# Two sequence blocks side by side through the mixers, and their w_out as seven block products

## The chip, the cores and the metric

The kernel runs on one core of a Trainium2 chip. The metric is the device time of one execution in microseconds (us), as the median of several. Profiled executions give a span (first to last instruction of the core), a little shorter than the device time.

## The reference

One decoder layer, batch 1, 2048 rows (tokens), width 1024, float32:

```
h = RMSNorm(x);  u = h @ W_in                        (1024 -> 3584)
gate_b, gate_c, v (512 each), x_r, g (1024 each) = split(u)
y_conv = gate_b * conv3(gate_c * v)                  (causal, per channel)
xr     = conv4(x_r) + bias                           (causal, per channel)
y_rnn  = RG-LRU(xr) * gelu(g)                        (16 heads of 64: two sigmoid gates
                                                      by block-diagonal products, then a scan)
x = x + concat[RMSNorm(y_conv), RMSNorm(y_rnn)] @ W_out    (1536 -> 1024)
x = x + relu(RMSNorm(x) @ W1)^2 @ W2                 (1024 -> 4096 -> 1024)
out = RMSNorm(x)
```

The scan and the convolutions run along the rows, so each block of rows needs the state that the block before left.

## The kernel before

The 2048 rows are four blocks of 512 (TB). A product is done in three passes: each factor is split into a rounded part (hi, on ScalarE) and a rest (lo, on VectorE, `split_into`, L180 to L182), and hi x hi, hi x lo and lo x hi are summed in PSUM. A matmul instruction takes 128x128 weights and 512 columns. PSUM has four tiles of 128x2x512, which all stages share.

Blocks are taken in pairs. The second pair (blocks 2 and 3) goes side by side: `pair_before_mlp` runs `mixers2`, then w_out, and both blocks form the halves of one matrix, so that seven products of half size replace eight (Strassen's form as Winograd wrote it; `ORDER` gives their order). For w_in and for w_out the kernel needs sums of the weights' quarters, as hi and lo parts. `prepare_sums` and `prepare_out_sums` make them one step at a time (`step`, the generator `background`) and put them in DRAM, in block 1's mixers (18 steps: `BG_UNITS`, `BG_STEPS`) and in the first pair's MLP. The MLP of each pair (`mlp`, lines L857 and L975) also uses seven products.

The first pair (blocks 0 and 1) goes one block after the other. `mixers(b, h)` walks through 14 units of w_in of 256 columns: x0 to x3 and g0 to g3 (recurrent), c0, c1, v0, v1, b0, b1 (conv). A unit is 48 matmuls (`mm_cols`, L240). `take` hands out a unit's pieces, loads and splits those two units ahead, and with `put_by` stores the split pieces in DRAM, from where block 1 and the second pair read them (`load_unit`, `In.load`). Between the units stand the recurrent chains, one for each pair of 128 channels (`pr` 0 to 3): `lru_take`, `lru_conv`, `lru_split`, `lru_gates` (12 small matmuls into `psri`, L692, then sigmoids), `lru_scan`. The first block's first three units are written out by hand before it (`start_x`, L486 to L546).

Meanwhile `next_part(b, n)` prepares the row factors of a later block: n = 0 to 3 load x (L1205) and square it (L1213), 4 takes the root, 6 forms a diagonal, 8 spreads it over the columns with two matmuls (`spread`, L449). `next_scale` multiplies the transposed x by the factors (L459) and `next_split` splits it into `h`.

`w_out_rows` and `w_out_conv` then multiply by w_out with the plain form: 12 groups of 24 matmuls in each block (`mm_rows`, L267), the factors of the norms put on the results on the rows' side. `turn` transposes the normed rows for the MLP (L1742).

`WOut.multiply` (L1889) is the seven-product w_out of the second pair. There the conv part's factor relative to the recurrent one is spread over the columns (`quotient`, `spread`), since both parts share a product.

Order: in `mixers` and the old w_out a planner orders each engine's instructions (program order is the priority; it takes what its cost model finds ready) and gives out the tile slots: 27 in `tp` (`temp`), 15 in `wp` (weights), 3 wide ones in `xp`, 2 in `hp`. In the second pair's part before the MLP, TensorE, ScalarE and VectorE are in program order, and in the MLP TensorE alone (`manual_schedule`). Nearly all transfers are issued in the queue of SP.

Of the kernel before, what the change touches and what calls it, by code (L numbers as in the profile page):

```python
# [15 lines left out]
P = 128  # L16
# [16 lines left out]
OUT_AHEAD = 2  # L33
# [7 lines left out]
BG_UNITS = 24  # L41
BG_STEPS = 2
# [22 lines left out]
def block_kernel(  # L65
# [5 lines left out]
    norm_mlp_g,  # L71
# [57 lines left out]
    def src_row(w, row):  # L129
        v = w[row : row + 256, :].rearrange("(j p) n -> p j n", p=P)  # L130
        return [v[:, 0:1, :], v[:, 1:2, :]], (P, 1, D)

    def src_quad(w, row):
        v = w[row : row + 512, :].rearrange("(h j p) n -> p h j n", p=P, j=2)
        return [
            v[:, i, :, 512 * c : 512 * c + 512] for i in range(2) for c in range(2)
        ], (P, 2, 512)

    units = []
    PAIRED = 2  # L140
    UNITS = ("x0", "g0", "x1", "c0", "g1", "x2", "v0", "g2", "x3", "b0", "g3", "c1", "v1", "b1")
    COLS = dict(x=COL_X, g=COL_G, c=COL_C, v=COL_V, b=COL_B)
    for b in range(PAIRED):
        for nm in UNITS:
            units.append((nm, src_col(w_in, COLS[nm[0]] + 256 * int(nm[1]))))
        for pr in range(4):
            units.append(("oB%d" % pr, src_row(w_out, 512 + 256 * pr)))
        for pr in range(2):
            units.append(("oA%d" % pr, src_row(w_out, 256 * pr)))
# [3 lines left out]
    NU = len(UNITS) + 6  # L153
    cache = {}

    def put_by(u, tiles):

        cache[units[u][0]] = []
        for part in tiles:
            row = []  # L160
            for t in part:
# [74 lines left out]
    def mm_cols(ps, w, h, j, lo=0, hi=TB, ks=range(KD)):  # L236
        for k in ks:
            pl = passes(w, h)
            for i, (ws, hs) in enumerate(pl):
                nc.tensor.matmul(  # L240
                    ps[:, j, lo:hi],
                    ws[k // 4][:, k % 4, j * P : (j + 1) * P],
                    hs[:, k, lo:hi],
# [3 lines left out]

    made = {}

    def col_unit(nm, h, ahead=AHEAD):  # L250
        if nm in made:
            return made.pop(nm)
        w = take(nm, ahead)
        if BG_UNITS <= cursor[0] < BG_UNITS + 9:
            for _ in range(BG_STEPS):
                step()
# [5 lines left out]

    def mm_rows(ps, y, w, j, t, first, final):
        pl = passes(y, w)
        for i, (ys, ws) in enumerate(pl):
            for half in range(2):
                nc.tensor.matmul(  # L267
                    ps[:, half, :],
                    ys[:, j, t * P : (t + 1) * P],
                    ws[j][:, 0, half * 512 : (half + 1) * 512],  # L270
                    start=first and i == 0,
                    stop=final and i == len(pl) - 1,
                )

# [123 lines left out]
    def norm_tile(b, t, g):  # L398
        ss = small("ss")
        rs = small("rs")[:, 0:1]  # L400
        xs = temp("xs")
        for i in range(2):
            nc.scalar.activation(
                xs[:, i, :], x_half(b, t, i), AF.Square, accum_out=ss[:, i : i + 1]
            )
        V.tensor_add(ss[:, 0:1], ss[:, 0:1], ss[:, 1:2])
        root = rstd_of(rs, ss[:, 0:1], 1)
        for i, sl in enumerate(HALF):
            V.scalar_tensor_tensor(xs[:, i, :], x_half(b, t, i), rs, g[:, sl], MUL, MUL)
        return xs, root  # L410

# [42 lines left out]
    def spread_rows(rs, n):  # L454
        return spread(diagonal(rs, n), n)

# [9 lines left out]

    def to_h(xs, h, t, parts=1):
        ps = psum("tps", (P, KD, P))
        for k in range(KD):
            nc.tensor.transpose(ps[:, k, :], xs[:, k // 4, k % 4 * P : (k % 4 + 1) * P], ident)  # L470
# [1958 lines left out]
```

## Time and profile before

| what | value |
|---|---|
| median of 3 runs | 2107.11 us (2106.87 to 2107.33) |
| profiled execution | 2106.28 us, span 2104.5 us |
| TensorE busy | 2096.0 us, 9396 matmuls |
| VectorE busy | 1603.7 us, 1848 instructions |
| ScalarE busy | 1104.2 us |
| transfers | 493 MB, 234 GB/s |
| granted TensorE clock | 0.999 |
| first block until its w_out ends | about 237 us |
| first pair until its MLP alone is left | about 486 us |

How to read it: a group of the profile is one line of the kernel on one engine with the tiles it writes and reads (out<-in), its count, its busy time in all, the mean of one, and the idle time of the engine just before its instructions with what ended it. A row of busy time by stretch gives the stretch, its length, the busy time of PE (TensorE matmul), PEld (weight load), DVE (VectorE), ACT (ScalarE) and POOL (GpSimd) with the instruction counts in brackets, the granted clock, the share of the DMA engines and GB/s; asked for one line, it shows the engines of that line only. Times of a chain start at the span's start.

### The profile page before, as it was taken

How to read it: one execution, taken by the hardware profiler on the slowest of the kernel's cores; microseconds unless marked ns; L12 is line 12 of the kernel's file. 1: busy time of each engine (PE TensorE's matmuls, PEld its weight loads, DVE VectorE, ACT ScalarE, POOL GpSimd, SP SyncE). 2: the span in 40 equal slices, each digit the busy share in tenths (PEclk: the TensorE clock that was granted, in tenths of full speed). 3: DMA queues.
4: the chain of work that ended last, by engine and by line, in shares of the span. 5: the costliest groups of instructions: out<-in, count | busy, mean ns of one | idle time of the engine just before them, and what ended most of it. 6: DMA issues, size and time to landing. Idle time of an engine off the chain costs nothing.

```text
span 2104.5 us, 25165 instructions
## 1 busy us (share of the span) xinstructions
PE 2096.0 (100%) x9396; PEld 1726.4 (82%) x9396; DVE 1603.7 (76%) x1848; ACT 1104.2 (52%) x1438; POOL 54.8 (3%) x71
## 2 busy tenths in 40 slices
PE   9999999999999999999999999999999999999998
PEld 7888888888888888888888887888888888888887
DVE  6889538858775777999997876785886765887776
ACT  6875447726554554444455888234764333333344
POOL 0110000000000000000000100000000000000000
PEclk9999999999999999999999999999999999999999
DMA  9988889743667778689564656775343355854432
GB/s 340 333 307 326 316 327 352 283 174 111 239 251 255 274 286 333 236 315 338 210 259 169 216 207 230 266 266 208 121 166 134 145 185 208 310 178 155 140 120 81
DMA packets 204762, 492.98 MB, mean 234 GB/s; under 512 B 15840, under 2 KB 80352, under 8 KB 204640
## 3 DMA queue, kind: packets, MB, share of 16 engines
q1 hardware_dynamic: 203040, 486.65, 63.9%
q10 hardware_dynamic: 1568, 4.72, 0.6%
q8 instruction: 74, 1.21, 0.2%
q14 instruction: 48, 0.39, 0.1%
q0 software_dynamic: 32, 0.00, 0.0%
HBM read 324.59 MB, written 166.72 MB: 233 GB/s over the span
## 4 chain that ended last, share of the span: by engine, by line
PE 99%; DVE 1%; ACT 0%; issue 0%; POOL 0%; ACTq 0%; POOLq 0%
PE up L857 42%; PE dn L975 28%; PE po L267 6%; PE ps_g L240 4%; PE wo_x L1889 3%; PE ps_x L240 3%; PE ps_v L240 2%; PE ps_b L240 2%; PE ps_c L240 2%; PE wo_w L1889 2%; PE wo_y L1889 1%; PE tps L1742 1%; PE psri L1498 1%; PE psri L692 1%; PE start_x L518 1%; PE start_x L240 1%
## 5 line engine op out<-in xcount | busy, mean ns | idle before, releaser
L857 PE MATMUL up<-H,w_hi 128*128 128x512 f32 x2576 | 795.0, 390 | 0.0
L857 PEld LDWEIGHTS up<-H,w_hi 128*128 128x128 f32 x2576 | 482.3, 188 | 102.5 <-issue 1.8
L857 PE MATMUL up<-H,w_lo 128*128 128x512 f32 x1288 | 501.5, 389 | 0.0
L975 PE MATMUL dn<-w_hi,z_hi 128*128 128x512 f32 x864 | 336.1, 389 | 0.0
L975 PE MATMUL dn<-w_lo,z_hi 128*128 128x512 f32 x864 | 336.1, 389 | 0.0
L975 PE MATMUL dn<-w_hi,z_lo 128*128 128x512 f32 x864 | 336.1, 389 | 0.0
L857 PEld LDWEIGHTS up<-H,w_lo 128*128 128x128 f32 x1288 | 241.7, 188 | 51.4 <-DVE w_lo L182 0.9
L181 ACT CAST z_hi<-z 128x1024 fp32r<-128x1024 f32 x112 | 118.0, 1053 | 306.3 <-PE dn L975 213.7
L182 DVE TENSOR_TENSOR w_lo<-w,w_hi 128x1024 fp32r<-128x1024 f32 x156 | 190.4, 1222 | 68.1 <-ACT w_hi L181 25.8
L181 ACT CAST w_hi<-w 128x1024 fp32r<-128x1024 f32 x156 | 162.5, 1049 | 131.4 <-PE up L857 52.6
L975 PEld LDWEIGHTS dn<-w_lo,z_hi 128*128 128x128 f32 x864 | 162.2, 188 | 33.9
L975 PEld LDWEIGHTS dn<-w_hi,z_lo 128*128 128x128 f32 x864 | 162.2, 188 | 33.7
L975 PEld LDWEIGHTS dn<-w_hi,z_hi 128*128 128x128 f32 x864 | 162.2, 188 | 33.4
L1007 DVE TENSOR_TENSOR x<-dn,x 128x1024 f32<-128x1024 f32 x108 | 131.1, 1222 | 23.2 <-PE dn L975 23.0
L182 DVE TENSOR_TENSOR z_lo<-z,z_hi 128x1024 fp32r<-128x1024 f32 x112 | 136.7, 1220 | 3.0 <-ACT z_hi L181 3.0
L869 ACT COPY snap<-up 128x1024 f32<-128x1024 f32 x48 | 48.7, 1015 | 73.9 <-PE up L857 73.4
L874 ACT ACTIVATE snap<-snap 128x1024 f32<-128x1024 f32 x33 | 35.1, 1062 | 75.7 <-DVE snap L894 26.5
L182 DVE TENSOR_TENSOR w_lo<-raw,w_hi 128x1024 fp32r<-128x1024 f32 x44 | 53.3, 1221 | 12.1 <-ACT w_hi L181 9.7
L1889 PE MATMUL wo_x<-w_o,y_hi 128*128 128x512 f32 x192 | 59.8, 392 | 0.0
L267 PE MATMUL po<-w_hi,y_hi 128*128 128x512 f32 x192 | 59.6, 393 | 0.0
L267 PE MATMUL po<-w_hi,y_lo 128*128 128x512 f32 x192 | 59.4, 390 | 0.0
L267 PE MATMUL po<-w_lo,y_hi 128*128 128x512 f32 x192 | 59.2, 389 | 0.0
(425 smaller groups left out, 3290.1 us busy)
## 6 DMA issues: line engine op xcount, KB each, us to landing
z<-d_z SPq DMA_DIRECT2D x112, 512.0 KB, 5.9
w<-in_w_mlp_in_dram SPq DMA_DIRECT2D x64, 512.0 KB, 5.9
d_z<-snap SPq DMA_DIRECT2D x64, 512.0 KB, 3.3
w_hi<-d_w SPq DMA_DIRECT2D x55, 512.0 KB, 6.4
w_lo<-d_w SPq DMA_DIRECT2D x55, 512.0 KB, 6.1
d_z<-z SPq DMA_DIRECT2D x48, 512.0 KB, 3.0
w<-in_w_mlp_out_dram SPq DMA_DIRECT2D x48, 512.0 KB, 8.8
d_w<-w_hi SPq DMA_DIRECT2D x40, 512.0 KB, 6.6
```

The costliest lines, as they stand in the source:

```text
L181: nc.scalar.copy(hi, src)
L182: return (lo_engine or V).tensor_tensor(lo, src, hi.bitcast(F32), SUB).ins
L240: nc.tensor.matmul(ps[:, j, lo:hi], ws[k // 4][:, k % 4, j * P : (j + 1) * P], hs[:, k, lo:hi], start=k == 0 and i == 0, stop=k == KD - 1 ...
L267: nc.tensor.matmul(ps[:, half, :], ys[:, j, t * P : (t + 1) * P], ws[j][:, 0, half * 512 : (half + 1) * 512], start=first and i == 0, stop ...
L518: nc.tensor.matmul(start_x[:, j], w[a][k // 4][:, k % 4, j * P : (j + 1) * P], h[c][:, k], start=k == 0 and n == 0, stop=k == KD - 1 and n ...
L692: nc.tensor.matmul(pr_[:, e, :], ws[own, c - gates[2], :], xsrc[own, j, :], start=i == 0, stop=i == 2)
L857: nc.tensor.matmul(ps[:, j, :], ws[:, k, j * P : (j + 1) * P], hs(k), start=i in (1, 2, 5) and k == 0 and n == 0, stop=k == 3 and n == len ...
L869: made_at["snap"] = nc.scalar.copy(t, ps).ins
L874: nc.scalar.activation(t, t, AF.Relu)
L975: nc.tensor.matmul(ps[t // 2][:, t % 2, :], zs[:, p, t * P : (t + 1) * P], ws[:, p, :], start=i in (1, 2, 5) and a == 0 and p == 0 and n == 0,
L1007: V.tensor_add(xt[b, th, dh], ps[th], xt[b, th, dh])
L1889: nc.tensor.matmul(ps[t // 2][:, t % 2, :], ys[:, j, t * P : (t + 1) * P], ws[:, j, :], start=first and n == 1, stop=final and n == 6 * le ...
```

## The change

Blocks 0 and 1 now go through the mixers side by side, but with plain products: a unit's pieces are loaded and split once and multiplied by block 0 and then by block 1 (`hold` keeps them). Block 1's scaled input is made at the start, as eight tiles `h1`, one for each quarter and part. The three units of the hand-written start are loaded a second time for block 1, as they were before. Of seven units, the halves of the pieces that the second pair doesn't read are no longer stored (`SECOND`).

w_out of the first pair takes the path of the second: `pair_before_mlp` serves both, and for the first pair it runs `pair_mixers` in place of `mixers2`. The seven w_out operands, the three plain ones among them, are all made by `prepare_out_sums`; its steps now run in the mixers of the first pair (`more(n)` does n of them), no longer in the MLP. Both pairs read all their w_out from there. The steps for w_in all run in the first pair's MLP. y of the recurrent part is scaled and spilled to DRAM and read back. The mixers of the first pair are still ordered by the planner; from `by_hand()` on, three engines are in program order. The MLP after it starts as the second pair's does.

The diff, cut:

```diff
+    UNITS = ("x0", "g0", "x1")
+    UNITS += ("c0", "x0", "g1", "g0", "x1", "x2", "v0", "g2", "x3", "b0", "g3", "c1", "v1", "b1")
+    SECOND = ("x1", "x3", "g1", "g3", "c1", "v1", "b1")
-    def mixers(b, h, early=None):
...
+    def pair_mixers(h, rest, st):
...
+        def unit(nm, n, hold=False):
+            if nm in made:
+                return made.pop(nm)
+            w = held.pop(nm, None) or take(nm)
+            if hold:
+                held[nm] = w
+            return col_unit(nm, hk[n], w)
...
+        def both(of, pr):
+            of(pr, 0, True)
+            of(pr, 1)
...
+        x_of(0, 0)
+        conv(0, 0)
+        load_xt(1)
+        for n in range(4):
+            next_part(1, n)
+        split(0, 0)
...
+        g_of(0, 0)
+        x_of(1, 0)
+        c_of(0, 0, True)
+        for n in (4, 6, 8):
+            next_part(1, n)
+        h1 = [[temp("h1", dt=F32R) for _ in range(4)] for _ in range(2)]
+        for q in range(4):
+            next_scale(1, q)
+            split_into(h1[0][q], h1[1][q], xtt[1, q])
+        hk.append(tuple((lambda k, t=t: t[k // 2][:, k % 2, :]) for t in h1))
+        gate(0, 0)
+        conv(1, 0)
+        scan(0, 0)
+        split(1, 0)
+        c_of(0, 1)
+        x_of(0, 1)
+        g_of(1, 0, True)
+        g_of(1, 1)
+        gate(1, 0)
+        conv(0, 1)
+        scan(1, 0)
+        split(0, 1)
+        g_of(0, 1)
+        x_of(1, 1)
+        more(2)
+        gate(0, 1)
+        conv(1, 1)
+        scan(0, 1)
+        split(1, 1)
+        both(x_of, 2)
+        more(2)
+        gate(1, 1)
+        conv(2, 0)
+        scan(1, 1)
+        split(2, 0)
+        both(v_of, 0)
...
+        both(g_of, 2)
...
+        gate(2, 0)
+        conv(2, 1)
+        scan(2, 0)
+        split(2, 1)
+        both(x_of, 3)
+        more(3)
+        gate(2, 1)
+        conv(3, 0)
+        scan(2, 1)
+        split(3, 0)
+        both(b_of, 0)
...
+        both(g_of, 3)
+        more(3)
+        gate(3, 0)
+        conv(3, 1)
+        scan(3, 0)
+        split(3, 1)
+        for of in (c_of, v_of, b_of):
+            of(1, 0, True)
+            if of == c_of:
+                keep_gates()
+                gate(3, 1)
+                scan(3, 1)
...
+            more(3)
+        c_of(1, 1)
+        more(30)
+        rest(39)
+        rest(41)
+        v_of(1, 1)
+        rest(42)
+        rest(43)
+        rest(44)
+        b_of(1, 1)
+        rest(46)
+        rest(47)
+        rest(48)
...
     def prepare_out_sums():
...
+            put(1, g, split(b11), b11)
...
+            put(3, g, split(b22), b22)
...
+            put(2, g, split(b21), b21)
...
-    background = chain(prepare_sums(), prepare_out_sums())
+    background = prepare_sums()
+    out_background = prepare_out_sums()
...
     for b in range(0, NB, 2):
         ups = [Up(s, b < PAIRED) for s in range(NS)]
-        if b < PAIRED:
-            ysA, ysB, accA, accB = mixers(b, h)
...
+            xs, r0, r1, g, order = pair_before_mlp(b, ups, by_hand)
+        r1, t2, rest = turns(r0, r1, g, order)
+        with tc.manual_schedule(engines={nc.tensor.engine}):
+            mlp(b, ups, r0, r1, t2, rest, xs, {0: (0, 1), 1: (2, 3)}, 3)
```

`rest(n)` is a function of `pair_before_mlp`: 39 fetches y, 41 to 44 take the recurrent part's factors, form the first sums and splits of y and load the first w_out operands, 46 to 48 take the conv part's factor.

More of the change, by code (lines that the diff above doesn't have):

```diff
@@ L32 @@
 AHEAD = 2
-OUT_AHEAD = 2
 LEAD1 = 2
@@ L160, in put_by @@
             row = []
-            for t in part:
+            for k, t in enumerate(part):
+                if k == 0 and units[u][0] in SECOND:
+                    row.append(None)
+                    continue
                 d = dp.tile(list(t.shape), F32, name="d_w")
@@ L246, in mm_cols, with whole, col_unit @@
                 )
+    def whole(h):
+        return tuple((lambda k, t=t: t[:, k, :]) for t in h)
     made = {}
-    def col_unit(nm, h, ahead=AHEAD):
-        if nm in made:
+    def col_unit(nm, h, w=None):
+        if w is None and nm in made:
             return made.pop(nm)
[L253 to L256, printed above, removed]
+        w = w or take(nm)
         ps = psum("ps_" + nm[0])
@@ L2384 @@
+_INS = ["x", "w_in", "w_out", "w_mlp_in", "w_mlp_out", "final_norm_g",
         "x_t", "rows_t", "gate_w", "mlp_g_t"]
```

438 lines of the change are left out of this document (129 added, 309 removed).

## The prediction

> **What bounds the kernel now.** I read the page's totals and its clock line first, then the chain that ended last, then busy time by stretch.
>
> ```profile
> span 2104.5 us, 25165 instructions
> PE 2096.0 (100%) x9396; PEld 1726.4 (82%) x9396; DVE 1603.7 (76%) x1848; ACT 1104.2 (52%) x1438; POOL 54.8 (3%) x71
> PEclk9999999999999999999999999999999999999999
> ```
>
> TensorE is busy for the whole span at full clock. Only fewer or cheaper products can shorten it, and every wait newly put on TensorE lengthens it. The chain of waits, in order of time (start, duration, what), says what a product costs:
>
> ```profile
> 6.26 11.57 PE start_x L518 x48
> 51.00 1.58 PE psri L692 x9
> 156.16 10.88 PE ps_b L240 x48
> 167.04 16.33 PE po L267 x72
> 183.37 0.48 PE po L449 x2
> 184.78 0.80 PE po L618 x8
> ...
> 480.81 294.05 PE up L857 x1296
> ...
> 1398.70 16.32 PE wo_x L1889 x72
> 2086.34 0.02 issue
> ```
>
> From 6.26 to 2086.34 us the chain never leaves TensorE. 72 products of 128x512 take 16.33 us in the old w_out (L267) and 16.32 us in the seven-product form (L1889): 226.8 ns each. The groups print another number:
>
> ```profile
> L267 PE MATMUL po<-w_hi,y_hi 128*128 128x512 f32 x192 | 59.6, 393 | 0.0
> ```
>
> 393 ns is one product from start to end; neighbours overlap, so the price of one more or one less is 226.8 ns.
>
> **The change part by part.** *w_out of blocks 0 and 1.* Products of the old form (two blocks) and of the seven-product form (pair 2 and 3), by stretch and line, count in brackets:
>
> ```profile
> 167.00:238.00 71.00, 66.64 (x288) 53.44 (x287) 1.00 0.84 311
> 398.00:474.00 76.00, 66.93 (x288) 53.51 (x287) 1.00 0.52 192
> 1364.00:1486.00 122.00, 116.63 (x504) 93.86 (x504) 1.00 0.61 213
> ```
>
> The first two are L267, 576 products; the third is L1889, 504 (7 block products x 4 row tiles x 18). The first pair takes over the form of the second: 72 products fewer, 72 x 0.2268 = 16.33 us. Added is the spreading of the conv factor over the columns, once for each block, two matmuls in 0.48 us (the row at 183.37 has this shape): +0.96 us. The statistics (0.80 us for eight records), the transposes, the gate products and the 28 w_in products are as many as before. So TensorE's own work falls by 15.4 us. In the trace of before that form ran in pair 2 without a TensorE wait between 1364 and 1486 us, and the code that orders it is the same, so I charge no wait inside it.
>
> The Trainium skill, "TensorE: Matmul & The Clock Gate", section "Back-to-back issue gap", gives N/2.4 + 2.5 ns, 216 ns for 512 columns. By it the 72 products would be worth 15.5 us. The trace has 226.8 ns, and the measurement decides.
>
> *w_in pieces loaded once.* The second block's 68 reloads, and stores of halves that nobody reads again, go:
>
> ```profile
> w_hi<-d_w SPq DMA_DIRECT2D x34, 512.0 KB, 7.7
> w_lo<-d_w SPq DMA_DIRECT2D x34, 512.0 KB, 7.0
> SPq L1327 <- ACT sum_hi L181: 28.8, 6, 9.8
> ```
>
> No TensorE wait named a transfer before, so this gains nothing. The queue of SP gets 42 stores and 42 loads of w_out sums instead, and 8 spills and 8 fetches of y. A store of a sum waits on SP for its rounding, up to 9.8 us in the third row, and a load of w_in behind it is late by as much. The cover is the load of pieces two units ahead: a unit now feeds both blocks, 2 x 10.88 = 21.8 us of TensorE. I charge nothing. POOL's halo and state copies stay 8 and 8.
>
> *The sums move.* The w_out sums, 24 VectorE operations in the MLP before, become 12 sums and 21 roundings in the mixers. In exchange the 18 steps of w_in sums that ran in block 1 go to the MLP: 63 steps in 67 places there, 66 before. The MLP's load is unchanged. In the mixers it is not, and there VectorE is the next engine. Busy time by stretch (length; PE, PEld, DVE, ACT, POOL):
>
> ```profile
> 0.00:25.00 25.00, 23.86 (x105) 19.69 (x106) 12.04 (x17) 17.92 (x34) 2.07 (x14) 1.00 0.97 339
> 0.00:167.00 167.00, 165.86 (x747) 135.09 (x748) 132.57 (x183) 126.66 (x171) 19.16 (x25) 1.00 0.92 328
> 25.00:225.00 200.00, 200.00 (x911) 163.60 (x910) 172.57 (x246) 132.25 (x169) 20.15 (x14) 1.00 0.90 326
> 237.00:398.00 161.00, 161.00 (x734) 131.33 (x733) 98.65 (x139) 101.59 (x148) 10.22 (x10) 1.00 0.90 337
> 1079.00:1364.00 285.00, 285.00 (x1301) 231.61 (x1300) 217.77 (x260) 193.07 (x231) 20.48 (x31) 1.00 0.64 231
> ```
>
> The two blocks' mixers hold 132.57 + 98.65 = 231.2 us of VectorE work. Prices for what comes and goes:
>
> ```profile
> L182 DVE TENSOR_TENSOR w_in<-w_in,sum_hi 128x1024 fp32r<-128x1024 f32 x6 | 7.3, 1222 | 2.6 <-ACT sum_hi L181 2.6
> L459 DVE SCALAR_TENSOR_TENSOR xT<-xT,prm,bcs 128x512 f32<-128x512 f32 x8 | 5.9, 750 | 0.0
> L182 DVE TENSOR_TENSOR h_lo<-xT,h_hi 128x1024 fp32r<-128x1024 f32 x4 | 4.9, 1218 | 0.0
> L1461 DVE TENSOR_TENSOR acc<-acc,v 128x512 f32<-128x512 f32 x6 | 4.2, 692 | 0.2
> L608 DVE TENSOR_TENSOR v<-v 128x1024 f32<-128x1024 f32 x6 | 7.3, 1222 | 0.1
> ```
>
> 33 operations of 1.222 us for w_out add 40.3. Block 1's scaled input and its split, which lay behind the old w_out, add 5.9 + 4.9 = 10.8. Row sums of squares add 24 x 0.69 = 16.6 for 8 of 1.222 (9.8): +6.8. Two y sums and four y splits at the end add 7.3. Sixteen operations for the w_in sums of block 1 go: -19.6. That is 277 us; work that crosses the edges of my stretches I take as even.
>
> TensorE's time for the mixers, without waits: 6.3 + 11.6 + 27 x 10.88 + 8 x 1.58 + 4 x 0.48 + 0.8 = 327 us. VectorE would be busy 277/327 = 85%; after the start (12.04 us in the first 25) 265/302 = 88%. Between 25 and 225 us it ran 172.57/200 = 86% while TensorE never waited. Taking that as what it can sustain, 265/0.863 = 307: TensorE waits 5 us. The ends are 0 (four PSUM slots and two units ahead absorb it) and 34 us, by the 217.77/285 = 76% of pair 2's mixers (277/0.764 = 362, less 327, is 35; rounded). I take 5: the row at 86% is the same code, planned in the same way, with the same splits. ScalarE had 126.66 + 101.59 = 228 us; 21 roundings, 16 scalings and four splits more, less what leaves, bring an estimated 265, 81%, still behind VectorE.
>
> *Block 1's first product.* It now stands at about 53 us, not 237 (x0, g0, x1, c0 of block 0, then the gates at 51.00). Before it: loads of x, 8 squares, root, diagonal, spread, scaling, split.
>
> ```profile
> 26.14 0.15 DVE L422 TENSOR_TENSOR s<-s,s 128x4 f32<-128x4 f32 x1
> 27.84 0.29 DVE L431 TENSOR_SCALAR diag_hi<-ident,rs_x 128x128 fp32r<-128x128 f32 x1
> 29.92 0.35 DVE L432 SCALAR_TENSOR_TENSOR diag_lo<-ident,rs_x,diag_hi 128x128 fp32r<-128x128 f32 x1
> 28.14 4.77 SPq L176 DMA_DIRECT2D raw<-in_w_in_dram  x4
> 49.13 1.01 SPq L1205 DMA_DIRECT2D xq<-in_x_dram  x2
> xq<-in_x_dram SPq DMA_DIRECT2D x12, 512.0 KB, 6.4
> L1213 ACT ACTIVATE xq<-xq 128x512 f32<-128x512 f32 x24 | 14.8, 621 | 3.8 <-DMA xq<-in_x_dram 3.8
> ```
>
> The program puts these loads right after the first convolution, so SP should issue them from about 33 us, behind the w_in loads at 28.14. From issue: 6.4 to land, 8 x 0.62 = 5 for the squares, 1.7 for the root and 2.4 for the diagonal (the same steps of block 0, from 26.14 to 27.84 and on to 30.27), 0.5 to spread, 1.5 + 2.3 for the first quarter's scaling and split: about 20 us, and with some queueing ready at 54 to 58. Behind the waiting product on TensorE stand the rest of block 1's first units and g1 of block 0. g1 (10.88 us) doesn't need block 1; its w_in piece came split before 52 us, and the planner may place it first. Ends: 0 and 11 us; I take 0, for that cover. If the cover is missing, the scaling of the later quarters is late next.
>
> **Sum.** -15.4 + 5 + 0 = -10.4 us. The profiled execution took 2106.28 us (span 2104.5), 0.8 under the median of 2107.11; against the median 2096.7, and I say 2096.
>
> **The rivals.** A difference of under 0.2% (4.2 us) can't be told from none here; that is 2102.9 to 2111.3.
>
> *VectorE doesn't keep up, slower.* Place: the PSUM of x, g, c, v and b units in the mixers waits for VectorE. Price by the 76% row: +34 - 15.4, 2126. It decides from a density below 277/(327 + 15.4) = 81%. For it: VectorE idles in the chains (sigmoids before the gated product) even in pair 2's mixers, and the planner sets this order, not a hand-written one. Against: at 76% and 61% (237 to 398) it had nothing more to do, since TensorE did not wait.
>
> *Block 1's input is late and not covered, no change.* +11 on top of the sum's first and second terms as far as they don't overlap: 11 to 15 us of waits, 2103 to 2107. For it: 49.13 was where x was asked for before. Against: that place was set by program order, not by lack of slots.
>
> A rule that would make such a wait dearer is the clock gate: the start shows a cold product.
>
> ```profile
> L486 PE MATMUL start_x<-ones_raw x12: 421/421/580, 1.1 to 3.6; 128*128 128x128 f32 x12
> L488 PE MATMUL start_x<-ones_raw x12: 274/421/421, 3.9 to 6.0; 128*128 128x128 f32 x12
> ```
>
> 421 ns falls to 274 some 4 us after the start. One restart after a long gap would repeat a few us of that, at most 2 more: this stays inside the second rival. The Trainium skill, same page, section "Part 1: The HAM clock gate", says that an idle window of about 3.4 us halves the clock until a busy one has passed; the start agrees, but no gap in this trace shows the return.
>
> *The saving is the whole 15.4.* 2091 to 2093, if all waits hide; part of my forecast's own range. *No saving, or a larger one by 393 ns a product:* 2107.1 - 28.3 + 1.6 = 2080; the chain's rows exclude it.
>
> **Chances.** Waits of 0 to 11 us (2091 to 2103): 0.68; waits of 11 to 20 (late input, or VectorE slightly short): 0.15; more (VectorE): 0.17. Hence faster 0.68, same 0.15, slower 0.17. The likeliest's own range is 2091 to 2103; the range for 8 in 10 runs from 2090 to 2111, which leaves out most of the slower cases.
>
> **What would show it.** Right: 504 products on the w_out line in each pair, 68 more records gone from TensorE; the first pair's w_out ending some 10 us earlier than 486; few waits of TensorE, all before 330 us, behind VectorE or block 1's split; DVE at 9 tenths there. Wrong: TensorE waits of over 15 us for PSUM emptied by VectorE; a gap at 50 to 65 us; w_out sums read from DRAM before they are stored; or waits in the MLP.

## The result, and the profile after

| kernel | median | ratio to before, 95% interval |
|---|---|---|
| before | 2106.99 us (2106.70 to 2107.33) | |
| after | 2157.43 us (2157.13 to 2158.20) | 1.024 [1.0222, 1.0258] |

The change makes the kernel 50 us slower. The forecast was 2096, in a range from 2090 to 2111. All medians here and below are of executions at the usual clock; one execution of one experiment's kernel (one block after the other, early diagonals), 2367.65 us at a granted clock of 0.842, is left out. The profiled execution of after took 2158.2 us. From its page, against the first fence of the prediction:

```profile
span 2156.4 us, 25019 instructions
PE 2096.5 (97%) x9328; PEld 1722.2 (80%) x9328; DVE 1623.7 (75%) x1860; ACT 1127.9 (52%) x1493; POOL 62.0 (3%) x71
```

TensorE has 68 records fewer, as forecast, and yet it is busy for as long as before (2096.5 against 2096.0), and now it is idle for 59.9 us (2156.4 - 2096.5), where it was for 8.5. The difference of the spans, 51.9, parts into 15.4 us of products saved, 51.4 us more idle time, and a rest of 15.9 us, by which the products that are left take longer (2096.5 against 2096.0 - 15.4 = 2080.6): -15.4 + 51.4 + 15.9 = 51.9. The rest can be checked: in five stretches before 402 us the granted clock is 0.50, and they hold 28.9 us of products (the rows stand in the last section), which at full clock would take 14.4 us less.

The chain that ended last says where it is lost (start, duration, what):

```profile
397.92 10.92 PE wo_x L1820 x41
...
531.75 294.42 PE up L746 x1296
...
1415.07 0.48 PE wo_y L408 x2
1415.55 10.93 PE wo_x L1820 x48
...
1549.78 283.48 PE up L746 x1248
```

The MLP alone begins at 531.75; before it began at 480.81. So 50.9 of the 51.9 us are lost before it. Almost 6 of them are lost in the first pair's w_out, which begins ahead of the rows shown here:

```profile
391.39 0.72 PE L1820 MATMUL wo_x<-w_o,y_hi 128*128 128x512 f32 x2
```

Seven of its products run from 391.39 us. Then it waits 3.75 us for the diagonal of the quotient, and the next 41 products take 10.92 us, where 48 of the second pair's take 10.93. In all it lasts 140.4 us (391.39 to 531.75), that of the second pair 134.7 (1415.07 to 1549.78). What TensorE waited for, in the whole execution (us in all, times, longest):

```profile
PE bc L408 <- DVE diag_hi L390: 14.2, 2, 11.7
PE psri L597 <- ACT xr_hi L167: 12.0, 2, 6.1
PE bc L408 <- DVE l_s L526: 11.2, 1, 11.2
PE ps_x L226 <- DVE s L583: 4.7, 1, 4.7
PE wo_y L408 <- ACT diag_hi L399: 3.8, 1, 3.8
PE psri L597 <- DVE xr_lo L168: 2.4, 2, 1.7
PE ps_b L226 <- DVE xr_in L545: 1.4, 1, 1.4
```

And the first instruction behind each long stop, from the timeline of TensorE (the bracket holds the idle time ahead of it):

```profile
62.72 0.77 PE L408 MATMUL bc<-diag_hi,ones_r 128*128 128x512 f32 x1 [11.21 <-DVE l_s L526]
211.01 0.79 PE L226 MATMUL ps_x<-h_hi,w_hi 128*128 128x512 f32 x1 [4.67 <-DVE s L583]
240.33 1.22 PE L597 MATMUL psri<-xr_hi,gate_hi 64*128 64x512 f32 x4 [5.85 <-ACT xr_hi L167]
311.61 1.22 PE L597 MATMUL psri<-xr_hi,gate_hi 64*128 64x512 f32 x4 [6.11 <-ACT xr_hi L167]
327.33 0.77 PE L408 MATMUL bc<-diag_hi,ones_r 128*128 128x512 f32 x1 [11.73 <-DVE diag_hi L390]
331.03 0.77 PE L408 MATMUL bc<-diag_hi,ones_r 128*128 128x512 f32 x1 [2.50 <-DVE diag_hi L390]
397.02 0.51 PE L408 MATMUL wo_y<-diag_hi,ones_r 128*128 128x512 f32 x1 [3.75 <-ACT diag_hi L399]
```

The first is the spread of block 1's factor, which the planner did not put behind g1 of block 0. The others stand where a recurrent chain or the factors of blocks 2 and 3 have to hand something to TensorE. The last is the quotient. Only one of the long ones, at 211, is a PSUM tile that VectorE had not emptied. The stop that ends at 311.61 can be followed back through both other engines:

```profile
303.69 1.23 DVE L608 TENSOR_TENSOR gi<-gi,xr 128x1024 f32<-128x1024 f32 x1 [3.53 <-ACT gi L605]
310.51 1.04 ACT L167 CAST xr_hi<-xr 128x1024 fp32r<-128x1024 f32 x1 [2.85 <-DVE xr L563]
```

Between the taps of one chain's convolution, VectorE has the gated product of the chain before (L608) in its order, and there it stands 3.53 us for ScalarE's sigmoids. ScalarE can round xr only after the last tap (L563), and TensorE's gate product starts behind the rounding. The stop that ends at 240.33 has the same form, with 5.21 us at L608. By stretch (PE, PEld, DVE, ACT, POOL, clock, transfers):

```profile
60.00:160.00 100.00, 96.28 (x428) 76.79 (x430) 70.89 (x101) 71.93 (x83) 5.75 (x5) 0.96 0.54 192
160.00:260.00 100.00, 86.35 (x370) 68.88 (x367) 72.00 (x92) 68.08 (x105) 15.29 (x10) 0.91 0.66 235
260.00:397.00 137.00, 112.23 (x492) 90.39 (x490) 108.45 (x141) 77.68 (x94) 13.16 (x7) 0.90 0.64 245
```

VectorE is 71 to 79% busy and ScalarE 57 to 72%, less than the 86% that VectorE had before without a TensorE wait. But these are means, and they hide full stretches:

```profile
180.00:200.00 20.00, 20.00 (x90) 16.57 (x89) 19.96 (x25) 7.68 (x9) 2.40 (x3) 1.00 0.49 166
220.00:240.00 20.00, 14.49 (x64) 11.65 (x63) 11.16 (x18) 19.47 (x33) 0.74 (x1) 0.95 0.54 209
260.00:280.00 20.00, 20.00 (x90) 16.56 (x89) 19.79 (x23) 15.11 (x18) 7.20 (x3) 1.00 0.43 141
```

No engine is full over 100 us, but VectorE is full from 180 to 200 and from 260 to 280 us, ScalarE from 220 to 240, and between such stretches each of them stands waiting for the other. A full engine alone does not make a stop: before, VectorE was busy for all of 160 to 200 us without a TensorE wait, beside w_out.

### The profile page after: what moved, and what is told of

It is laid out like the page before. It is cut to its first block, busy times and chain, and to the rows that moved or that the text cites. A ratio compares the mean times of both kernels' runs of the same rounds, so it can differ in the third digit from the quotient of the medians.

```text
span 2156.4 us, 25019 instructions
## 1 busy us (share of the span) xinstructions
PE 2096.5 (97%) x9328; PEld 1722.2 (80%) x9328; DVE 1623.7 (75%) x1860; ACT 1127.9 (52%) x1493; POOL 62.0 (3%) x71
## 4 chain that ended last, share of the span: by engine, by line
PE 78%; DVE 2%; ACT 1%; issue 1%; DMA 0%; SPq 0%; DVEq 0%; ACTq 0%
PE up L746 40%; PE dn L864 26%; PE wo_x L1820 5%; PE wo_w L1820 3%; PE wo_y L1820 2%; PE psri L1494 1%; PE dn L883 1%; PE tps L1707 0%; DVE x L920 0%; DMA z<-d_z 0%; ACT r L1714 0%; DVE w_lo L168 0%; DVE z_lo L168 0%; DVE H L2086 0%; DVE x L1833 0%
## 5 line engine op out<-in xcount | busy, mean ns | idle before, releaser
L1820 PE MATMUL wo_x<-w_o,y_hi 128*128 128x512 f32 x384 | 121.0, 396 | 0.0
L1820 PEld LDWEIGHTS wo_x<-w_o,y_hi 128*128 128x128 f32 x384 | 71.7, 190 | 14.7 <-DVE x L1833 0.4
L1820 PE MATMUL wo_x<-w_o,y_lo 128*128 128x512 f32 x192 | 75.6, 394 | 0.0
L1820 PE MATMUL wo_w<-w_o,y_hi 128*128 128x512 f32 x192 | 59.1, 389 | 0.0
L168 DVE TENSOR_TENSOR w_lo<-t,w_hi 128x1024 fp32r<-128x1024 f32 x32 | 39.0, 1219 | 18.6 <-PE dn L864 14.3
```

The costliest lines, as they stand in the source:

```text
L168: return (lo_engine or V).tensor_tensor(lo, src, hi.bitcast(F32), SUB).ins
L1820: nc.tensor.matmul(ps[t // 2][:, t % 2, :], ys[:, j, t * P : (t + 1) * P], ws[:, j, :], start=first and n == 1, stop=final and n == 6 * le ...
```

## The experiments

Five theories came up. 1: inputs come late at the head of an in-order queue (loads and squares of x on ScalarE, diagonals on VectorE, block 1's input). 2: VectorE and ScalarE have no room for the work that was moved into the mixers. 3: each stop also costs slowed clock. 4: w_out of a block used to lie beside the next block's chains and hid their lag. 5: the recurrent chains stand too near each other on TensorE. All runs below are medians, with the kernel before run beside them (2106.94 to 2107.31 us).

| kernel | median | ratio, 95% interval |
|---|---|---|
| without x of blocks 2 and 3 | 2147.04 | 1.0189 [1.0174, 1.0204] |
| factors of blocks 2 and 3 in the MLP | 2147.01 | 1.0187 [1.0170, 1.0204] |
| without the arithmetic of the sums | 2137.99 | 1.0147 [1.0132, 1.0163] |
| one block after the other | 2161.43 | 1.0255 [1.0240, 1.0271] |
| the same, early diagonals | 2161.63 | 1.0258 [1.0238, 1.0279] |
| after, early diagonals | 2163.74 | 1.0268 [1.0253, 1.0284] |
| after, reordered | 2161.00 | 1.0254 [1.0239, 1.0269] |
| reordered, factors in the MLP | 2138.79 | 1.0152 [1.0137, 1.0167] |
| the same, without the sums' arithmetic | 2118.16 | 1.0053 [1.0038, 1.0068] |
| the same, sums on GpSimd | 2156.08 | 1.0234 [1.0218, 1.0249] |
| the same, chains evenly spaced | 2137.06 | 1.0143 [1.0128, 1.0158] |
| one after the other, without the sums' arithmetic | 2146.67 | 1.0184 [1.0167, 1.0201] |
| reordered and MLP, casts on VectorE | 2143.69 | 1.0176 [1.0159, 1.0193] |
| reordered and MLP, tap on ScalarE | 2142.46 | 1.0169 [1.0154, 1.0184] |
| before, doubled sums of w_in | 2133.06 | 1.0122 [1.0107, 1.0137] |
| before, more VectorE work | 2129.93 | 1.0111 [1.0094, 1.0128] |
| before, more ScalarE work | 2120.86 | 1.0068 [1.0053, 1.0083] |
| before, more transfers | 2128.06 | 1.0098 [1.0083, 1.0113] |

**Taking work out, and undoing half of the change.** Four kernels, from after. Without x of blocks 2 and 3 (factors formed from block 1's sums):

```diff
-        if n < 4:
+        if n < 4 and b > 1:
+            nxt["s2"] = factors[1]["kept"]
+        elif n < 4:
```

> Leaves out the 16 loads and 16 squares of x of blocks 2 and 3 during the first pair's mixers; their factors are formed from block 1's sums instead, so that roots, diagonals and spreads stay where they are, and the rows of blocks 2 and 3 come out with a wrong scale. Theory 1 (late heads of in-order queues): the stops at 206 and 234 to 241 us (4.7 + 5.8 + 1.7 + 1.4 us), which begin with ScalarE waiting for a load of x, go, with about 4 us of slowed clock; the stop for block 2's diagonals (11.7 + 2.5) may stay or shrink: 2130 to 2145 us. The stop at 51 us stays. Theory 2 (VectorE and ScalarE are short of throughput because of the sums of w_out): VectorE loses nothing here, so most of the stops stay: 2147 to 2157 us. Theory 3 (clock): TensorE's busy time falls by about 0.3 us for each microsecond of idle time that goes.

The factors' parts in the MLP's first products, by a table of places:

```diff
-        for k in (2, 3):
-            next_part(k, 0)
...
+                for k, part in LATE.get((s, i), ()):
+                    next_part(k, part)
```

> The loads, squares, roots, diagonals and spreads for the factors of blocks 2 and 3 are made in the MLP of the first pair instead of in its mixers; everything is still computed. Theory 1: all stops between 200 and 331 us that hang on these (4.7, 5.8, 3.1, 6.1, 14.2: 34 us) go, and some 10 us of slowed clock with them, while the MLP has room for the work: 2108 to 2122 us; the 11 us at 51 us and the 3.75 at 393 stay. Theory 2: the sums of w_out still crowd VectorE in the mixers, so that only the 4.7 us with ScalarE's loads go: 2140 to 2155 us. Theory 3: TensorE busy about 2086 instead of 2096.5.

Without the sums' arithmetic:

```diff
-            split_into(hi, src.bitcast(F32R), src)
-            return hi
+            return src
...
-            for t in (hi.bitcast(F32), src):
+            for t in (src, src):
```

> Leaves out the arithmetic on w_out in the mixers: its pieces are stored as they are, with the same transfers, and the 33 VectorE and 21 ScalarE instructions that form the sums and their two parts are gone, so the values of the first pair's w_out products are wrong. Theory 2: with about 40 us less on VectorE and 22 us less on ScalarE the stops behind 200 us go: 2105 to 2120 us. Theory 1: the heads of the queues are still the loads, squares and diagonals of blocks 2 and 3, and little changes: 2143 to 2157 us. Both leave the 11 us at 51 us.

The mixers of block 0, then those of block 1, with the seven-product w_out:

```diff
+    UNITS = ("x0", "g0", "x1", "c0", "g1", "x2", "v0", "g2", "x3", "b0", "g3", "c1", "v1", "b1") * 2
+    SECOND = ()
...
+        for n in range(2):
+            x_of(0, n)
+            conv(0, n)
+            split(0, n)
...
```

> The mixers of block 0, then those of block 1, each with its own loads of the w_in pieces as in the kernel before; the pair's w_out stays one product of seven block products, and its sums are still made during these mixers. Everything is computed. Theory 1: no input is needed early, the stop at 51 us is gone, and what is left is the 72 products saved: 2091 to 2097 us against 2107. Theory 2: the sums crowd VectorE in this order too, and 20 us or more of stops for PSUM or for a factor stay: 2108 to 2130 us.

Measured: 10.4, 10.4 and 19.4 us less than after for the first three, and 4.0 us more for the fourth. In the first, the stops at 234 to 241 us are gone, as theory 1 said, but the one at 305 grew from 6.1 to 9.4 us, and the time lies at the edge of theory 2's range. Theory 1 had promised 35 to 49 us for the second and misses it, though the stops between 200 and 332 us fell from 34.0 to 13.6 us. Others grew or came: one at the quotient (6.9 us), and one in the MLP for split weights (6.6 us), beside 9.5 us that were left at the gate products.

Theory 2 had promised 37 to 52 us for the third and gets half. Theory 3 has the sign right and the size wrong: for each microsecond of idle time that went, TensorE's busy time fell by 0.79, 0.35 and 0.46 us in the three kernels, where it had 0.3. The fourth falsifies theories 1 and 2 as they were priced: the order of the old mixers does not bring the old time back. So going side by side is not the cause by itself.

**Moving the stops.** In the fourth kernel, TensorE waited 33.4 us for two diagonals; in the kernel before the first of these was ready at 157 us for a spread at 183, which stood inside w_out. This gave theory 4, and three kernels that only change places:

```diff
             for k in (2, 3):
                 next_part(k, 4)
+                next_part(k, 6)
...
-                    next_part(k, 6)
```

> As the kernel of one block after the other, but the diagonals of the next block's factors are formed right after their roots, some 60 us earlier in VectorE's order; nothing is left out. Theory 4 (new): w_out of each block used to lie between the root and the spread of the next block's factor; without it TensorE reaches the spread while VectorE, in order, still works on older chains. Then the stops of 21.2 and 12.3 us at the two spreads go and slowed clock of some 10 us with them: 2112 to 2125 us against 2161. Theory 2 (VectorE is short of throughput): the same work is still due, the stops only turn up at the next product or eviction: 2145 to 2161 us.

> As the changed kernel, but the diagonals of blocks 2 and 3 are formed right after their roots; nothing is left out. Theories 1 and 4 (place in the queue): the stops of 11.7 and 2.5 us at 316 to 331 us go with some 4 us of slowed clock: 2134 to 2144 us against 2157; the stops at 51, 206, 234 and 305 us stay. Theory 2: 2150 to 2158 us, the 14 us come back at another wait.

```diff
-    UNITS += ("c0", "x0", "g1", "g0",
+    UNITS += ("c0", "g1", "x0", "g0",
...
+        g_of(1, 0, True)
+        next_part(1, 8)
...
-        for of in (c_of, v_of, b_of):
-            of(1, 0, True)
+        both(c_of, 1)
...
+        rest(46)
         b_of(1, 1)
-        rest(46)
```

> The changed kernel with only the order of its steps changed: block 1's x is loaded for its squares before the transposed x; g1 of block 0 is multiplied before the spread of block 1's factor and block 1's first unit; the diagonals of blocks 2 and 3 right after their roots; c1 of both blocks ahead of the last recurrent chain; the quotient of w_out begun ahead of the last unit. Nothing is left out, VectorE and ScalarE do the same work. Theories 1 and 4: the 11.2, 14.2 and 6 to 9 us stops and the 3.8 us at the quotient go, 10 to 20 us of small ones stay: 2095 to 2115 us. Theory 2: no less than 2135 us, as the work due is the same.

The last of this group joins the reordered kernel with the table of places above:

> As the reordered kernel, but the loads, squares, roots, diagonals and spreads of blocks 2 and 3 lie in the first pair's MLP. Nothing is left out. Theories 1 and 4: what is left of the stops at ScalarE's loads of x between 200 and 240 us goes as well, the MLP gets 5 to 8 us of stops at its weights' splits on ScalarE: 2095 to 2112 us, within 6 us of the reordered kernel. Theory 2: 2130 us or more.

The stops went from where they were, and came back elsewhere. In the kernel of one after the other the 33.4 us were at two diagonals. Here is the longest wait of TensorE when these come early, and then what after with early diagonals waits for, beside 11.0 us at block 1's spread, as in after:

```profile
PE psri L596 <- ACT xr_hi L166: 23.5, 2, 21.6
```

```profile
PE psri L597 <- ACT xr_hi L167: 16.9, 2, 11.4
PE ps_c L226 <- DVE s L583: 8.3, 1, 8.3
```

None of the three is faster than its parent: +0.2 for the first, +6.3 for the second and +3.6 for the reordered one against after. Theories 1 and 4, by which places alone make the stops, are gone; the first two kernels also lie above the ranges of theory 2. Only where work left the mixers did the time fall: the reordered kernel with the factors in the MLP takes 2138.79, 22.2 less. Places are not without effect, though: with the factors in the MLP and the old order it was 2147.01, so there the reordering gains 8.2 us, where it cost 3.6 in after.

**How much room there is.** From that kernel, the sums' arithmetic left out again (the same edit), the sums on another engine, and the gate products about three units apart:

> As the reordered kernel with the factors of blocks 2 and 3 in the MLP, and besides without the arithmetic of the sums of w_out in the mixers: pieces are stored as they are, with the same transfers, so the first pair's w_out has wrong values. Theory 2 (in these mixers VectorE and ScalarE, which hand work to each other, have no more room): 54 instructions less give 15 to 25 us, 2112 to 2124 us. Theory 4 (only places in the queues): 2132 to 2140 us, as with the sums.

```diff
-        tt = V.tensor_tensor
+        tt = nc.gpsimd.tensor_tensor
...
-            split_into(hi, src.bitcast(F32R), src)
+            split_into(hi, src.bitcast(F32R), src, nc.gpsimd)
```

> As the reordered kernel with the factors in the MLP, but the 33 VectorE instructions of the sums of w_out run on GpSimd, which is 3% busy; nothing is left out. Theory 2: if GpSimd does one in some 2 to 4 us, and takes nothing from VectorE meanwhile, the time is near that without the sums, 2115 to 2130 us. If GpSimd slows VectorE or the sums come late to w_out: 2140 to 2170 us. Theory 4: 2134 to 2142 us.

```diff
+        x_of(2, 0, True)
         gate(0, 1)
...
-        both(x_of, 2)
+        x_of(2, 1)
+        v_of(0, 0, True)
         gate(1, 1)
...
```

> As the reordered kernel with the factors in the MLP, but the recurrent chains' gate products stand about three units apart on TensorE (34 us), where they stood two to four units apart; nothing is left out and the work is the same. Theory 5 (each chain needs some 30 us of VectorE and ScalarE in turn, so that two units apart are too near): stops of 10 to 20 us go, 2115 to 2130 us. Theory 2: the work in the stage is the same and so is the time, 2133 to 2145 us.

And the arithmetic left out, by the same edit, in the kernel of one block after the other with early diagonals:

> As the kernel of one block after the other with early diagonals, without the arithmetic of the sums of w_out: pieces are stored as they are, with the same transfers, so the first pair's w_out has wrong values. Theory 2: without the 54 instructions the mixers are nearly those of the kernel before, which had no stop: 2100 to 2125 us against 2162. Theory 4 (w_out of each block was the work that hid the lag of the chains, and it is gone): 2135 to 2160 us.

Without the arithmetic 20.6 us go, as 19.4 did from after and as 15.0 go with one block after the other. On GpSimd the sums cost 17.3 us more; the last section shows what they do to VectorE. The pages of the kernel with the sums (span 2136.7 us) and of that without (2115.6 us):

```profile
PE 2096.4 (98%) x9328; PEld 1723.2 (81%) x9328; DVE 1624.9 (76%) x1860; ACT 1128.7 (53%) x1493; POOL 71.8 (3%) x71
```

```profile
PE 2090.5 (99%) x9328; PEld 1719.5 (81%) x9328; DVE 1588.4 (75%) x1827; ACT 1110.9 (53%) x1472; POOL 49.6 (2%) x71
```

TensorE's idle time, span less busy time, falls by 15.2 us (40.3 to 25.1), its busy time by 5.9. Even spacing changes little (2137.06): theory 5 is gone. One block after the other without the sums' arithmetic is still 40 us over the kernel before, where theory 2 had 2100 to 2125. It lies in the range of theory 4, which had lost as a theory of places; the test of it in another form comes below. Its TensorE also waits for split weights (8.0 us) and for w_out from DRAM (6.1 us), with the DMA engines 96% busy from 160 to 260 us. I did not separate these.

**Which engine.** The 21 roundings from ScalarE to VectorE, and the first tap of the convolution from VectorE to ScalarE:

```diff
+            V.tensor_copy(hi, src)
+            V.tensor_tensor(src.bitcast(F32R), src, hi.bitcast(F32), SUB)
```

> As the reordered kernel with the factors in the MLP (2138.8 us), but the 21 roundings of the sums of w_out run on VectorE and no longer on ScalarE: VectorE gets about 15 to 25 us more, ScalarE 22 us less; nothing is left out. If VectorE sets the end of the mixers, 2148 to 2165 us. If ScalarE does, 2120 to 2135 us. If it is the handing over between the two, about the same or a little less, 2132 to 2142 us.

```diff
-            V.tensor_scalar(
+            nc.scalar.activation(
                 xr[:, j, :],
                 xr_in[:, j, 0:TB],
+                AF.Identity,
```

> As the reordered kernel with the factors in the MLP, but the first tap of the recurrent convolution (16 instructions of 0.54 us) runs on ScalarE and no longer on VectorE: VectorE gets 9 us less, ScalarE about 11 us more; nothing is left out. If VectorE sets the end of the mixers, 2126 to 2134 us. If ScalarE does, 2146 to 2155 us. If the handing over does (two more in each chain), 2138 to 2150 us.

Either way it gets 4 to 5 us slower. The first time lies between the ranges for the handing over and for VectorE, the second in that for the handing over. Neither is what one engine as the only bound would give, and neither engine gains the kernel time by taking over work from the other.

**The kernel before under load.** Theory 4 leaves a test: if w_out beside the mixers hid the lag, the old mixers would take more work at no cost.

```diff
-BG_STEPS = 2
+BG_STEPS = 4
```

> The kernel before with twice as many of its steps for the sums of w_in in block 1's mixers (36 where there were 18; the rest still in the MLP): 16 more VectorE and 8 more ScalarE instructions there, some 20 and 8 us, with their transfers. Nothing is left out. Theory 4 (w_out of the same block, done right behind its own mixers, lets the chains lag): within 4 us of the kernel before, 2104 to 2111 us. Theory 2 (VectorE's room in the mixers is all that counts; there it is 72 us busy in 100): 2115 to 2130 us.

They don't: +25.8 us for 16 VectorE and 8 ScalarE instructions and their transfers. Theory 4 is gone in this form too. Then each kind of load alone (18 VectorE instructions, 18 on ScalarE where the doubled sums had 8, or 27 transfers), in block 1's mixers, where the stretch from 237 to 398 us had VectorE 61% busy on average:

```diff
             for _ in range(BG_STEPS):
                 step()
+            for _ in range(2):
+                extra = temp("extra").rearrange("p a (b c) -> p (a b) c", c=P)
+                same = ident[:, None, :].broadcast_to([P, 8, P])
+                V.tensor_tensor(extra, same, same, SUB)
```

> The kernel before with some 16 more VectorE instructions of 128x1024 in block 1's mixers, two for each unit in the same places as the sums; they compute nothing that is used, read and write only on chip, and need no other engine. Nothing is left out. If VectorE's time alone makes the stops: 2120 to 2135 us, as the doubled sums did (2133). If it takes both engines and the handing over between them, or the sums' transfers: 2107 to 2114 us.

```diff
+                nc.scalar.copy(extra, ident[:, None, :].broadcast_to([P, 8, P]))
```

> As that, but with some 16 more ScalarE instructions of 128x1024 in place of those on VectorE. If ScalarE's time makes the stops: 2118 to 2135 us. If VectorE's alone does: 2107 to 2111 us. The doubled sums had 8 such instructions.

```diff
+            nc.sync.dma_start(
+                extra, w_in[0:256, 0:512].rearrange("(j p) n -> p j n", p=P)
+            )
+            for _ in range(2):
+                d = dp.tile([P, 2, TB], F32, name="d_extra")
+                nc.sync.dma_start(d, extra)
```

> The kernel before with one more load and two more stores of 0.5 MB for each unit in block 1's mixers, as the doubled sums have, and no arithmetic. Nothing is left out. If SP's order or the transfers make the stops: 2115 to 2135 us. If the engines' time does: 2106 to 2110 us.

All three cost: +23.0, +13.9 and +21.1 us, each in the range set for its own engine's time or for the transfers. The group of the added VectorE instructions, and that kernel's row from 237 to 398 us, to be held against the 98.65 us of VectorE in the prediction's row:

```profile
L260 DVE TENSOR_TENSOR extra<-ident x18: 1201/1220/1225, 257.7 to 398.8; 128x1024 f32<-128x1024 f32 x18
```

```profile
237.00:398.00 161.00, 149.38 (x657) 120.28 (x657) 103.93 (x131) 86.14 (x128) 11.66 (x9) 0.95 0.85 310
```

By the row of before, VectorE had 62 us free for 22 us of work, and yet it did only 5 us more in the stretch. But that row is a mean. Here it is in two parts, and behind it the end of the stretch in the kernel with the added instructions:

```profile
237.00:300.00 63.00, 63.00 (x290) 51.78 (x289) 18.81 (x32) 27.73 (x52) 0.38 (x2) 1.00 0.95 356
300.00:398.00 98.00, 98.00 (x446) 79.56 (x445) 79.84 (x109) 73.86 (x96) 9.85 (x8) 1.00 0.87 325
```

```profile
340.00:398.00 58.00, 51.28 (x219) 40.35 (x218) 55.79 (x72) 40.13 (x47) 4.58 (x3) 0.91 0.78 286
```

Sixteen of the 18 instructions run behind 316 us. There VectorE had 18 us free of 98, and they take 19.5; from 340 us on it is 96% busy. So VectorE's own time can explain this run. It does not explain the other two: between 300 and 398 us VectorE is busy for 69.1 us with the added ScalarE instructions and for 68.6 with the transfers, and TensorE stops. In the kernel with more transfers one stop can be followed through the timeline, from VectorE to ScalarE to TensorE:

```profile
373.95 1.23 DVE L1354 TENSOR_TENSOR w_in<-w_in 128x1024 f32<-128x1024 f32 x1 [8.33 <-DMA w_in<-in_w_in_dram]
```

```profile
382.37 1.04 ACT L181 CAST xr_hi<-xr 128x1024 fp32r<-128x1024 f32 x1 [8.60 <-DVE xr L664]
```

```profile
383.47 1.22 PE L699 MATMUL psri<-xr_hi,gate_hi 64*128 64x512 f32 x4 [4.98 <-ACT xr_hi L181]
```

VectorE stands for 8.33 us before a sum of w_in whose load is late. Behind that sum, in order, are the convolution's taps. ScalarE can round xr only after them, and TensorE's gate product waits for the rounding. The sum itself is needed by nobody for hundreds of microseconds.

**What is shown, and what stays open.** Shown: the saving on w_out is real (68 records); nearly all of the loss lies in the first pair's mixers; the arithmetic of the sums there is 15.0 to 20.6 us of it (19.4 from after itself), the factors of blocks 2 and 3 are 10.4 (22.2 in the reordered kernel); reordering without taking work out gives nothing; the kernel before was already so near the edge that each of the four loads added to its mixers cost 13.9 to 25.8 us. Open: the last 26 us, by which the reordered kernel without the factors and the sums' arithmetic in its mixers misses 2091.6 (2107 - 15.4). Its 16.6 us of added idle time are named by its trace: 5.5 in the MLP for split weights, 5.0 at the quotient, 3.6 at block 1's first product and 2.5 at gate products; 9.9 us more are slowed products. No run takes these away. Open too is how engine time, queue places and buffers share in the price of added load: the three loads sum to 58 us, while the doubled sums cost 25.8, and each of them also takes tile slots, which I did not separate. No run changes the number of slots, of which block 1's `h1` holds eight of 27 in these mixers, and none replaces the planner's order by one written by hand, as the second pair's mixers have, where VectorE is 76% busy and TensorE does not wait. Both could be part of the loss. A form in which only the first two w_out operands are made in the mixers and the others beside the products was not tried.

No kernel here beats the kernel before. The best that computes everything is the one with evenly spaced chains, 1.4% slower than it.

## Why the prediction was wrong

- *VectorE's density, +5 us:* this step failed. It took the 86% of one stretch without TensorE waits as a rate that VectorE can sustain, and means over hundreds of microseconds as what counts. In after, VectorE runs at 75% from 60 to 397 us (251.3 of 337), full for a while and then waiting for ScalarE, and the stops between 200 and 332 us come to 34.0 us (4.7 + 5.9 + 1.7 + 1.4 + 6.1 + 11.7 + 2.5) where the sum had 5. The stop-free stretch showed an order that happened to fit. In the kernel before, 16 instructions more where VectorE was 81% busy break it. ScalarE, put "behind VectorE" at an estimated 81%, counts by itself: 18 instructions on it cost 13.9 us in the kernel before.
- *The far end of that term, 34 us:* it agrees with the 34.0, and in part by luck. It came from the 76% of pair 2's mixers as a rate of VectorE alone; most of the stops are hand-overs between the engines and late factors. Even both far ends together fall short: -15.4 + 34 + 11 is 29.6 us, and the spans differ by 51.9. The slowed products (15.9) and the stop at the quotient (3.75) are most of the rest.
- *w_out, -15.4 us:* right in records. "No wait inside it" failed once: 3.75 us at the quotient and half clock behind it make it almost 6 us longer. The MLP has no wait, as said.
- *Block 1's first product, 0 us:* the other end came true. Its spread could start only at 62.7 us, where 54 to 58 were worked out; the planner placed it ahead of g1, and TensorE stood for 11.21 us. Giving it g1 as cover by hand left 3.6 us of waits there, but the mixers lost the gain again.
- *SP's queue, nothing charged:* not shown to be nothing. In the kernel before, 27 added transfers cost 21.1 us; what the queue costs in after no run separates.
- *The clock, at most 2 us more:* about right for one restart (4.3 us of products at half clock behind the first stop, 2.2 us lost), but there were five such stretches; 15.9 us in all.
- *The rivals:* "VectorE doesn't keep up" had the right sign and the wrong place. It named PSUM tiles that VectorE empties; that is 6.1 us of the waits (4.7 + 1.4). Most of the others are hand-overs within the chains and late factors. It gave 2126, at a chance of 0.17; and the second rival's late input came on top of it, not in its place.

## What to carry to other kernels

A profile row with a busy share and no waits is evidence of an order that fits, and not of room. Before charging little for work added to such a stretch, ask for rows as short as one chain (some 20 us here), since 61% on average was 30% and then 81%; count how many hand-overs lie between two products and what stands in order behind each added instruction; and put the far end of the range at the whole work added, more when the clock falls with each stop. The cheapest test is to add dummy work of the planned size in the old kernel: here 18 instructions that compute nothing used showed in one run that the old mixers charge 23 us for 22 us of it. And a saving of 0.7% on the bounding engine did not pay for 54 instructions of arithmetic moved from the MLP into these mixers, where leaving them out gains 19.4 us.

## What the runs showed of the hardware

Slowed clock. Around and behind stops the products run at half clock for some microseconds. The five stretches of after (length, PE, clock), and the products behind the last long stop:

```profile
53.60:67.20 13.60, 4.30 (x14) 0.50 0.89 358
210.60:214.00 3.40, 2.99 (x7) 0.50 1.02 418
237.90:251.50 13.60, 8.03 (x23) 0.50 0.64 211
309.60:336.80 27.20, 10.26 (x28) 0.50 0.35 113
398.40:401.70 3.30, 3.30 (x9) 0.50 1.05 420
```

```profile
331.00:336.70 5.70, 5.67 (x13) 0.50 0.94 301
```

13 records in 5.7 us, one in 0.43 where 0.227 is the rule. The last of the five stretches belongs to the stop of 3.75 us, and begins only after the products are running again, at 397.02:

```profile
392.00:398.30 6.30, 2.55 (x11) 1.00 1.02 406
```

The length of a stop alone does not settle it. In the reordered kernel with the factors in the MLP, one of 2.02 us that ends at 104.8 is followed by half clock (first row); in the kernel before with more ScalarE work, one of 2.84 us that ends at 356.8 is not (second row):

```profile
106.20:109.50 3.30, 3.30 (x12) 0.50 0.89 323
```

```profile
356.80:362.00 5.20, 5.20 (x23) 1.00 0.22 86
```

The Trainium skill, "TensorE: Matmul & The Clock Gate", section "Part 1: The HAM clock gate", names two states of this gate, full and half clock, the lower one after an idle window of some 3.4 us that runs freely. The rows show the same two states; that the window is not tied to the stop would fit the late begin, and the stop of 2.02 us is shorter than it. The page calls the ramp at the start less than 1% of a typical span; here five stretches make it 0.7%.

GpSimd beside VectorE. The sums on GpSimd took 2.8 to 3.0 us each, and slowed VectorE: the same VectorE instruction in the kernel with the sums on GpSimd, as a group (busy, mean ns) and with its shortest, median and longest ns, and then with the sums on VectorE:

```profile
L173 POOL TENSOR_TENSOR w_out<-w_out,sum_hi 128x1024 fp32r<-128x1024 f32 x12 | 35.9, 2999 | 9.5 <-ACT sum_hi L172 9.3
L638 DVE TENSOR_TENSOR s<-v,s 128x1024 f32<-128x1024 f32 x8 | 14.1, 1765 | 0.2
L638 DVE TENSOR_TENSOR s<-v,s x8: 1212/1224/3405, 99.9 to 356.0; 128x1024 f32<-128x1024 f32 x8
```

```profile
L638 DVE TENSOR_TENSOR s<-v,s 128x1024 f32<-128x1024 f32 x8 | 9.8, 1221 | 0.1
```

Most of the eight ran at the old speed, and single ones took nearly three times as long. VectorE had 33 instructions (40 us) less and was busy 12.2 us longer (1637.1 against 1624.9). The Trainium skill, "Perfetto Trace Analysis", section "Optimizing Scalar/DVE Operations", says that the two share a read port of SBUF, so that moving work between them might not help. The trace agrees that it did not: the run was 17.3 us slower. The port itself no row shows.
